# Two attention branches in a hybrid block: row blocks of four first-branch and seven second-branch heads issued side by side

## The chip, the cores and the metric

The kernel runs on one core of a Trainium2 chip. The engines of the core are named as the profile names them: PE (TensorE, matrix products into PSUM), DVE (VectorE), ACT (ScalarE, functions by table and copies), POOL (GpSimd) and SP (SyncE, which here only issues DMAs). Each engine works through its own instructions in a fixed order; waits between engines are semaphores. The metric is the device time in microseconds.

## The reference

One layer on 2048 frames of 1024 channels. After a norm and one wide projection, two attention branches run on the same input: stick-breaking attention (first branch, "sb") and latent attention with softmax (second branch, "mla"), 8 heads each. Sigmoid gates merge them.

```
h = rmsnorm(x, norm_in_g[l]);  proj = h @ w_in[l]     # split into nine parts
# first branch, 8 heads of 64:
z = q_sb k_sb^T * scale
log_beta = log_sigmoid(z);  log_1m = where(strict, log_sigmoid(-z), 0)
later = cumsum(log_1m, reverse=True) - log_1m
o_sb = where(strict, exp(log_beta + later), 0) @ v_sb
# second branch, 8 heads of 96 (64 and 32 rotated), values of 64:
p = softmax(where(allowed, z, -inf));  o_mla = p @ v_mla
y = g_sb * ((o_sb * silu(gate_sb)) @ w_o_sb) + g_mla * ((o_mla * silu(gate_mla)) @ w_o_mla)
out = rmsnorm(x + y @ w_out)
```

## The kernel before

Frames are taken in reverse order, in 16 row blocks of 128, so a row block `i` attends to the 16 - i key blocks from i on (`chunks`: one chunk of up to 1024 keys for i of 8 and more, two chunks before that). Every factor of a matmul is split into a high and a low half of 16 bits, and a product is three matmuls (`gemm`).

The work has four kinds.

- *Norms.* `norm_x` brings x, scales it, splits it and turns it by a DMA transpose into hT, which stays in SBUF as two halves (big0, big1).
- *Dense steps.* `dense_stream` is a generator of 224 steps, each one row block of one 384-column piece of the wide projection (24 matmuls into a PSUM tile mm of a ring of two): four pieces for the first branch's heads (sb), the second branch's queries (mq) and keys (mk) with a second, smaller product each (up-projection), and eight gate pieces (g). The weights of a piece are prepared ahead (`prep_w`, `bound_of`), with a round trip through DRAM for a maximum. When mk is done, its row buffers are closed and their memory becomes the pool `more`.
- *Heads.* `sb_units` computes, for each chunk, scores z (PSUM, two tiles of 1024 columns), two Sigmoids on ACT into U and B, a running product over U on DVE (`stick`, one chunk late), their product into B, then in `weigh` the high and low halves into a tile hl, a DMA transpose of hl into hlT, and values on PE one chunk late (two, once `more` is open: `run_third`). `mla_units` computes scores once for the row maximum, once turned with the maximum taken off, Exp on ACT into U or B, halves into a tile pt, and values. pt shares the rings of hl and hlT.
- *Closing stage.* `gated`, `merge` and `finish`, for 16 row blocks: gates, the two output products, the last product (1536 matmuls of 512 columns in all) and the last norm. Its weights `W["o"]` and `W["w"]` are split by `resident` into the places of the two halves of hT.

The order: 16 dense steps with the norms, then the 16 heads one after another, the first branch's eight first. `PLAN` says how many dense steps a head carries, spread over its row blocks:

```
PLAN = [17] * 8 + [8] * 7 + [4]
```

So the first branch's heads carry 136 steps and the second's 60; 12 are left, and are written behind the heads. This is the order in which the program is written. A scheduler then sets the order in which each engine's instructions stand, within the limits of buffers and dependencies, and can move a step forward. POOL issues the gate stores (`gd<-go`, a ring of two go tiles) and clears the first column of every U.

Where ACT goes from Sigmoid to Exp or back, the built program has an instruction ACT_TABLE_LOAD in between.

Of the kernel before, what the change touches and what calls it, by code (L numbers as in the profile page):

```python
# [9 lines left out]
F32 = mybir.dt.float32  # L10
# [6 lines left out]
P = 128  # L17
S = 2048
# [13 lines left out]
MASK = -3.0e35  # L32
PLAN = [17] * 8 + [8] * 7 + [4]
SCALES = ("g", 4)
# [5 lines left out]
def block_kernel(tc, x, norm_in_g, w_in, w_ck, b_gate, q_norm_g, w_q_up, kv_norm_g, w_kv_up,  # L40
# [11 lines left out]
    with ExitStack() as ctx:  # L52
# [131 lines left out]
        with ExitStack() as tctx:  # L184
# [26 lines left out]
            def u_tile():  # L211
                return un.tile([P, 1028], F32, name="U", tag="U")

            def b_tile():
                return un.tile([P, 1024], F32, name="B", tag="B")

            def hl_tile(n):
                count[0] += 1
                pool, bufs = (more[0], 2) if more and count[0] % 5 % 2 == 0 else (un, 2)
                return pool.tile([P, 2048], F16, name="hl", tag="hl", bufs=bufs)[:, 0:2 * n]  # L220

            def hlT_tile():
                pool, bufs = (more[0], 3) if more and count[0] % 5 % 2 == 0 else (un, 2)
                return pool.tile([P, 16, 128], F16, name="hlT", tag="hlT", bufs=bufs)

            def norm_x(i):
                xt = (b_tile() if i % 2 else u_tile())[:, 0:1024]
                SP.dma_start(out=xt, in_=x[i * P:(i + 1) * P, :])
                hl = (hlT_tile().rearrange("p a c -> p (a c)") if i % 2 else hl_tile(1024))
# [51 lines left out]

            def weigh(unit, vt, blk0, n, first, last, fill, done):


                run_third(2 if more else 1)
                hl = hl_tile(n)
                fill(hl[:, 0:n], hl[:, n:2 * n])
                nb = n // P
                t = hlT_tile()
                SP.dma_start_transpose(out=t[:, 0:2 * nb, :], in_=hl)  # L290
# [18 lines left out]
            def o_group(col):  # L309

                cur = {}

                def put(av, f, i):
                    if i % 4 == 0:
                        cur["t"] = kvp.tile([P, 4, 64], F32, name="ot", tag="ot", bufs=2)
# [6 lines left out]
            def halves(nm, *parts):  # L322

                out = []
                for a in range(2):
                    t = kvp.tile([P, 8, 130 if nm == "vt" else 128], F16, name=nm, tag=nm, bufs=3)
# [30 lines left out]
            def sb_units(h, pre):  # L357
# [4 lines left out]
                for i in range(NB):  # L362
# [5 lines left out]
                    for ci, (c0, n) in enumerate(cks):  # L368
# [8 lines left out]
                        def stick(U=U, B=B, n=n, ci=ci, c0=c0, i=i, unit=unit, last=(ci == len(cks) - 1)):  # L377
                            V.tensor_tensor_scan(out=U[:, 0:n + 1], data0=U[:, 0:n + 1], data1=U[:, 0:n + 1],  # L378
                                                 initial=unit["prev"] if ci else PS, op0=ALU.mult, op1=ALU.bypass)
                            unit["prev"] = U[:, n:n + 1]  # L380
                            V.tensor_tensor(out=B[:, 0:n], in0=B[:, 0:n], in1=U[:, 0:n], op=ALU.mult)  # L381
# [4 lines left out]

                            weigh(unit, vt, i + c0 // P, n, ci == 0, last, fill, lambda av: put(av, of, i))

# [155 lines left out]

            pt_count = [0]

            def pt_tile():

                pt_count[0] += 1
                k = pt_count[0] % (9 if more else 4)  # L550
                if k < 4:
                    pool, tag, bufs = un, "hl" if k % 2 else "hlT", 2
                else:
                    pool, tag, bufs = (more[0], "hl", 2) if k % 5 < 2 else (more[0], "hlT", 3)
                return pool.tile([P, 16, 128], F16, name="pt", tag=tag, bufs=bufs)

            lift, turn, last_av = deque(), deque(), deque()
# [11 lines left out]
            def mla_units(h, pre):  # L569
                mzc = pre[8]  # L570
                kh = halves("kt", (0, 64, mk_d[0:64, :, h, :]), (64, 128, mk_d[0:64, :, 8, :]))
                kl = halves("kl", (0, 64, mk_d[64:128, :, h, :]), (64, 128, mk_d[64:128, :, 8, :]))
                vt = halves("vt", (0, P, mv_d[:, :, h, :]))
                put = o_group(512 + h * 64)
                for i in range(NB):
                    if i % 4 == 0:
                        qt4 = kvp.tile([P, 2, 4, 128], F16, name="qt", tag="qt", bufs=2)
# [16 lines left out]
                    def row_max(mr=mr, qh=qh):  # L594

                        mt = ps_av()
                        with tc.issue_after(last_pe[0].ins):
# [3 lines left out]
                    def weights(i=i, cks=cks, qh=qh, ql=ql):  # L601
                        parts = []
                        for ci, (c0, n) in enumerate(cks):
# [258 lines left out]
            for i in range(NB):  # L862
                advance(1)
                if i + LEAD < NB:
                    norm_x(i + LEAD)
            for h in range(2 * H):
                if h == 2 * H - 1:
                    mla_stages(0, 0)
                    mla_stages(0, 0)
                    mctx.close()  # L870
                    more.clear()
                    tl.append(tctx.enter_context(tc.tile_pool(name="tl0", bufs=1, side="right", reuse_waits="tile")))
                if h == H:
                    run_second(0)
                    run_third(0)
                it = sb_units(h, pre["sb", h // 2]) if h < H else mla_units(h - H, pre["mk", 0])
                tot = sum(S - i * P for i in range(NB))
                cum, done = 0, 0
                for i, _ in enumerate(it):
                    cum += S - i * P  # L880
                    want = PLAN[h] * cum // tot
                    advance(want - done)
                    done = want
                    if h == 2 * H - 1 and i == EARLY:
                        gated(0)

# [73 lines left out]
```

## Time and profile before

| | |
|---|---|
| median of three runs | 2286.37 us (2282.97 to 2297.44) |
| the profiled execution | 2291.27 us |
| its span in the trace | 2289.5 us |
| mean granted clock of PE | 0.956 of full |
| busy: PE, DVE, ACT | 86%, 68%, 55% |

"Busy" is the time in which an instruction of that engine is under way. Matmuls are pipelined, so one that takes 0.33 us from start to end can start 0.16 us after the one before. At 1.00 of the clock PE runs at 2.4 GHz, at half of it at 1.2 GHz.

### The profile page before, as it was taken

To read this page: it belongs to the slowest core of one execution; us is meant where nothing else is said; L and a number is where in the kernel's file an instruction comes from. 1 tells how busy PE (TensorE), PEld (TensorE's weight loads), DVE (VectorE), ACT (ScalarE), POOL (GpSimd) and SP (SyncE) were. 2 spreads that over 40 slices of the span, in tenths; PEclk is the share of its full clock that TensorE was granted. 3 is DMA by queue.
4 is the path that set the end of the run, shared out by engine and by line. 5 is a ranking of instruction groups with operands and counts; after the bars stand their busy time and mean duration, and the time that the engine had idled before them with its cause. 6 is when DMAs were issued, how large, how long until landed. Compare 5 with 4: busy or idle time off the path is not lost.

```text
span 2289.5 us, 46188 instructions
## 1 busy us (share of the span) xinstructions
PE 1967.3 (86%) x18656; PEld 1252.5 (55%) x18656; DVE 1557.9 (68%) x2500; ACT 1265.4 (55%) x2116; POOL 277.8 (12%) x690
## 2 busy tenths in 40 slices
PE   3878888788767887999899999968999787999997
PEld 1545555445435544555557676755767675444443
DVE  3368778668766869887885554765565876766674
ACT  6456566555545657776654643775544777322321
POOL 1211111111111111112110101001010000000000
PEclk9989999999979999999999999998999998999999
DMA  9979888897988979888771522243252323866752
GB/s 249 225 132 156 157 153 160 160 153 159 185 167 157 207 169 169 172 158 168 130 173 48 149 63 72 61 125 87 63 149 67 110 71 80 256 194 185 200 157 74
DMA packets 666150, 330.21 MB, mean 144 GB/s; under 512 B 605776, under 2 KB 626000, under 8 KB 663888
## 3 DMA queue, kind: packets, MB, share of 16 engines
q1 hardware_dynamic: 645392, 272.19, 56.1%
q0 software_dynamic: 18432, 54.55, 8.5%
q8 instruction: 146, 2.39, 0.5%
q10 hardware_dynamic: 2112, 0.52, 0.1%
q14 instruction: 68, 0.56, 0.1%
HBM read 132.06 MB, written 71.90 MB: 89 GB/s over the span
## 4 chain that ended last, share of the span: by engine, by line
PE 47%; DMA 23%; DVE 13%; ACT 8%; issue 6%; SPq 1%; POOL 1%; ACTq 0%; DVEq 0%; POOLq 0%
DMA hlT<-hl 7%; PE mm L178 7%; PE mm L180 6%; PE mm L179 6%; PE z L344 4%; DVE U L378 4%; DMA rt<-r 3%; PE yo L178 2%; PE z L609 2%; PE yo L180 2%; PE yo L179 2%; PE z L613 2%; PE z L612 2%; DMA utb<-hlb 2%; PE y L178 2%
## 5 line engine op out<-in xcount | busy, mean ns | idle before, releaser
L178 PE MATMUL mm<-w,hT 128*128 128x384 f16 (+1 forms) x1792 | 590.2, 330 | 79.5 <-ACT w L166 37.0
L179 PE MATMUL mm<-w,hT 128*128 128x384 f16 (+1 forms) x1792 | 589.4, 329 | 0.8 <-DVE w L167 0.8
L180 PE MATMUL mm<-w,hT 128*128 128x384 f16 (+1 forms) x1792 | 589.0, 329 | 0.0
L378 DVE TENSOR_TENSOR_SCAN U<-U 128x1025 f32<-128x1025 f32 (+3 forms) x192 | 323.7, 1687 | 51.0 <-ACT U L374 49.5
L344 PE MATMUL z<-kt,qt 128*128 128x512 f16 x960 | 257.6, 362 | 58.4 <-DVE rt L432 13.2
L384 ACT CAST hl<-B 128x1024 f16<-128x1024 f32 (+3 forms) x192 | 152.4, 798 | 234.0 <-DVE B L381 131.2
L178 PEld LDWEIGHTS <-hT 128*128 128x128 f16 x1792 | 178.5, 100 | 155.7 <-DMA hT<-hl 25.3
L179 PEld LDWEIGHTS <-hT 128*128 128x128 f16 x1792 | 178.3, 99 | 148.4 <-issue 48.6
L180 PEld LDWEIGHTS <-hT 128*128 128x128 f16 x1792 | 178.3, 99 | 113.0 <-issue 9.2
L385 DVE TENSOR_TENSOR hl<-B,hl 128x1024 f16<-128x1024 f32 (+3 forms) x192 | 173.5, 909 | 87.9 <-ACT hl L384 87.4
L609 PE MATMUL z<-qt,kt 128*128 128x128 f16 x1088 | 205.0, 224 | 19.6 <-DVE mx L587 14.8
L587 DVE TENSOR_REDUCE mx<-z 128x1 f32<-128x1024 f32 (+3 forms) x192 | 173.6, 909 | 70.4 <-PE z L348 49.8
L613 PE MATMUL z<-qt,kl 128*128 128x128 f16 x1088 | 202.0, 224 | 0.0
L612 PE MATMUL z<-qt,kt 128*128 128x128 f16 x1088 | 202.0, 224 | 0.0
L299 PE MATMUL av<-vt,hlT 128*128 128x64 f16 x1088 | 124.4, 198 | 89.5 <-DMA hlT<-hl 87.3
L374 ACT ACTIVATE U<-z,nzc 128x1024 f32<-128x1024 f32 (+3 forms) x192 | 166.4, 867 | 39.4 <-PE z L344 38.7
L381 DVE TENSOR_TENSOR B<-B,U 128x1024 f32<-128x1024 f32 (+3 forms) x192 | 174.7, 912 | 15.6 <-ACT B L375 1.2
L375 ACT ACTIVATE B<-z,zc 128x1024 f32<-128x1024 f32 (+3 forms) x192 | 166.1, 867 | 3.1 <-DVE hl L385 3.0
L299 PEld LDWEIGHTS <-hlT 128*128 128x128 f16 x1088 | 103.8, 100 | 116.7 <-DMA hlT<-hl 106.8
L619 DVE SCALAR_TENSOR_TENSOR pt<-U,pt 128x1024 f16<-128x1024 f32 (+7 forms) x128 | 96.5, 755 | 90.4 <-ACT pt L618 89.8
L344 PEld LDWEIGHTS <-qt 128*128 128x128 f16 x960 | 87.3, 101 | 102.4 <-issue 45.1
L628 PE MATMUL av<-vt,pt 128*128 128x65 f16 x1088 | 127.0, 194 | 10.2 <-ACT qt L599 4.2
(258 smaller groups left out, 4367.2 us busy)
## 6 DMA issues: line engine op xcount, KB each, us to landing
gd<-go POOLq DMA_DIRECT2D x128, 192.0 KB, 3.3
wf<-in_w_in_dram SPq DMA_DIRECT2D x26, 768.0 KB, 5.6
gt<-gd SPq DMA_DIRECT2D x10, 1024.0 KB, 6.0
qkd<-rt POOLq DMA_DIRECT2D x32, 256.0 KB, 4.5
mqd<-rt SPq DMA_DIRECT2D x32, 256.0 KB, 2.7
qt<-mqd POOLq DMA_DIRECT2D x32, 256.0 KB, 3.5
wf<-in_w_out_dram SPq DMA_DIRECT2D x16, 512.0 KB, 4.2
xt<-in_x_dram SPq DMA_DIRECT2D x16, 512.0 KB, 3.6
```

Of the source, the lines that this page charges most:

```text
L178: T.matmul(out=ps, lhsT=xh(k), rhs=wh(k), start=(k == 0), stop=False)
L179: T.matmul(out=ps, lhsT=xh(k), rhs=wl(k), start=False, stop=False)
L180: last_pe[0] = T.matmul(out=ps, lhsT=xl(k), rhs=wh(k), start=False, stop=(k == kk - 1))
L299: T.matmul(out=av[:, 0:64], lhsT=t[:, j, :], rhs=v[:, 0:64], start=(first and j == 0), stop=False)
L344: last_pe[0] = T.matmul(out=z[:, s:s + c], lhsT=st, rhs=half[:, o + s // P:o + (s + c) // P, :].rearrange("p a b -> p (a b)"), start=(a == ...
L378: V.tensor_tensor_scan(out=U[:, 0:n + 1], data0=U[:, 0:n + 1], data1=U[:, 0:n + 1], initial=unit["prev"] if ci else PS, op0=ALU.mult, op1= ...
L381: V.tensor_tensor(out=B[:, 0:n], in0=B[:, 0:n], in1=U[:, 0:n], op=ALU.mult)
L385: V.tensor_tensor(out=lo, in0=B[:, 0:n], in1=hi, op=ALU.subtract)
L587: V.tensor_reduce(out=mx[:, ci:ci + 1], in_=z[:, 0:n], axis=AX.X, op=ALU.max)
L609: T.matmul(out=zj, lhsT=kh[b // 8][:, b % 8, :], rhs=qh, start=True, stop=False)
L612: T.matmul(out=zj, lhsT=kh[b // 8][:, b % 8, :], rhs=ql, start=False, stop=False)
L613: T.matmul(out=zj, lhsT=kl[b // 8][:, b % 8, :], rhs=qh, start=False, stop=True)
```

## The change

The heads are written in three stages in place of one list. Four first-branch heads run alone with 80 dense steps. After them the dense stream is advanced until `more` is open. Then the row blocks of the other four first-branch heads and of seven second-branch heads alternate, with 108 dense steps: `spread` takes the next row block from the stream that has done the smaller share of its work. The last second-branch head follows alone with four dense steps. 15 steps are written behind it.

To make room, the halves of the first branch's weights no longer have a tile hl: they lie over U, which is spent by then (1028 floats hold 2 x 1024 halves), so U stays in use until its transpose has landed. U has four buffers instead of three. Since U is overwritten, the last element of the running product is copied to a small tile pv for the next chunk. Turned tiles have two tags, hlT and pt, of two buffers each: alternating when one branch runs alone, one for each branch side by side. Values are two chunks late in the stage alone and one chunk late side by side (the reverse of before). The second branch's keys, values and queries come from `more` while both run, and the last head's low key halves lie over a U tile. `row_max` takes its PSUM tile from the dense steps' ring mm.

```diff
-PLAN = [17] * 8 + [8] * 7 + [4]
+ALONE, ALONE_STEPS = 4, 80
+BOTH_STEPS = 108
+LAST_STEPS = 4
...
-                return un.tile([P, 1028], F32, name="U", tag="U")
+                return un.tile([P, 1028], F32, name="U", tag="U", bufs=4)
...
+            def turned_tile(sb):
+
+                count[0] += 1
+                tag = ("hlT" if sb else "pt") if stage[0] == "both" else ("hlT", "pt")[count[0] % 2]
+                return un.tile([P, 16, 128], F16, name=tag, tag=tag, bufs=2)
...
-            def weigh(unit, vt, blk0, n, first, last, fill, done):
-
-
-                run_third(2 if more else 1)
-                hl = hl_tile(n)
+            def weigh(unit, hl, vt, blk0, n, first, last, fill, done):
+
+
+                run_third(1 if stage[0] == "both" else 2)
                 fill(hl[:, 0:n], hl[:, n:2 * n])
                 nb = n // P
-                t = hlT_tile()
+                t = turned_tile(True)
...
-                            unit["prev"] = U[:, n:n + 1]
+                            if not last:
+                                unit["prev"] = sm.tile([P, 1], F32, name="pv", tag="pv", bufs=3)
+                                V.tensor_copy(out=unit["prev"], in_=U[:, n:n + 1])
...
-                            weigh(unit, vt, i + c0 // P, n, ci == 0, last, fill, lambda av: put(av, of, i))
+                            weigh(unit, U.bitcast(F16)[:, 0:2 * n], vt, i + c0 // P, n, ci == 0, last, fill,
+                                  lambda av: put(av, of, i))
...
-                        mt = ps_av()
+                        mt = ps_mm()
...
-                            pt = pt_tile()
+                            pt = turned_tile(False)
...
-            for h in range(2 * H):
...
+            def heads(units, hs, key):
+                for h in hs:
+                    for i, _ in enumerate(units(h, pre[key(h)])):
+                        yield work(i)
+
+            def spread(streams, steps):
+
+
+                done, total, gone = [0] * len(streams), sum(t for _, t in streams), 0
+                while True:
+                    left = [k for k, (_, t) in enumerate(streams) if done[k] < t]
+                    if not left:
+                        break
+                    k = min(left, key=lambda k: done[k] / streams[k][1])
+                    done[k] += next(streams[k][0])
+                    want = steps * sum(done) // total
+                    advance(want - gone)
+                    gone = want
+                    yield
+                for it, _ in streams:
+                    next(it, None)
+
+            sb_key, mla_key = (lambda h: ("sb", h // 2)), (lambda h: ("mk", 0))
+            for _ in spread([(heads(sb_units, range(ALONE), sb_key), ALONE * whole)], ALONE_STEPS):
+                pass
+            while not more:
+                advance(1)
+            stage[0] = "both"
+            for _ in spread([(heads(sb_units, range(ALONE, H), sb_key), (H - ALONE) * whole),
+                             (heads(mla_units, range(H - 1), mla_key), (H - 1) * whole)], BOTH_STEPS):
+                pass
...
+            for i, _ in enumerate(spread([(heads(mla_units, [H - 1], mla_key), whole)], LAST_STEPS)):
+                if i == EARLY:
+                    gated(0)
```

What the scheduler makes of it is shown at three places. The first is SP, in the middle of the first-branch heads that run beside the projections (hl or U holds the halves, hlT and pt are turned tiles, rt belongs to the projections). Before:

```order
L290 DMA_TRANSPOSE hlT<-hl 128x14x128
L290 DMA_TRANSPOSE hlT<-hl 128x16x128
L445 DMA wf<-in_w_q_up_dram 128x3x384 x2
L290 DMA_TRANSPOSE hlT<-hl 128x12x128
L263 DMA_TRANSPOSE rt<-r 128x8x128
```

After:

```order
L290 DMA_TRANSPOSE pt<-U 128x16x128
L332 DMA vt<-vd_77 128x8x128
L290 DMA_TRANSPOSE hlT<-U 128x14x128
L264 DMA_TRANSPOSE rt<-r 128x8x128
L135 DMA wjunk<-bd_cq 128x128
L290 DMA_TRANSPOSE pt<-U 128x12x128
```

Four turned tiles take turns instead of two, and the source is U itself. The second place is ACT in the gate steps. Before, in a first-branch head, it has Sigmoids (U and B from z), the cast of the high half, the copy of an output (ot) and gate work (go, wjunk):

```order
L374 ACTIVATE U<-z,nzc_1387 128x1024
L375 ACTIVATE B<-z,zc_1386 128x1024
L384 CAST hl<-B 128x1024
L374 ACTIVATE U<-z,nzc_1387 128x768
L156 ACTIVATE wjunk,am<-wf 128x768
L384 CAST hl<-B 128x896
L317 ACTIVATE ot<-av,of_1388 128x64
L661 ACTIVATE go<-mm,gt_7989 128x384
```

After, side by side (the scale mzc marks the second branch's Exp, nzc and zc the Sigmoids):

```order
L378 ACT_TABLE_LOAD
L378 ACTIVATE U<-z,nzc_1287 128x896
L379 ACTIVATE B<-z,zc_1286 128x896
L662 ACTIVATE go<-mm,gt_9002 128x384
L600 CAST qt<-mm 32x128
L158 ACTIVATE wjunk,am<-wf 128x768 x2
L616 ACT_TABLE_LOAD
L616 ACTIVATE U<-z,mzc 128x768
L390 CAST U<-B 128x896
```

Sigmoid and Exp now alternate, each with its table load; the whole program has 112 of them, and had 8. The third place is ACT at the end of the heads, where the last weights (WHL from in_w_out, scale r_wout) are split. Before, they stand among the second branch's Exps:

```order
L172 ACTIVATE WHL_26363<-wf,r_wout 128x1024 x2
L615 ACTIVATE U<-z,mzc 128x1024
L599 CAST qt<-av 32x128
L317 ACTIVATE ot<-av,fo 128x64
L618 ACTIVATE pt<-U 128x1024
L615 ACTIVATE U<-z,mzc 128x896
L172 ACTIVATE WHL_26363<-wf,r_wout 128x1024
```

After:

```order
L806 ACT_TABLE_LOAD
L806 ACTIVATE gt<-gt 128x1024
L810 ACTIVATE gt<-gt 128x2048
L174 ACTIVATE WHL_26298<-wf,r_wout 128x1024 x2
L806 ACTIVATE w<-w 128x3072
L174 ACTIVATE WHL_26298<-wf,r_wout 128x1024 x4
L174 ACTIVATE w<-w,ra 128x1024
```

They moved behind the last Exp, between the gates of the closing stage's first blocks (gt and w). On PE the last 309 matmuls before the closing stage are dense steps in one row; before, the last dense step stood ahead of more than 1,900 matmuls of the heads.

## Rows read from the trace of the kernel before

**Rows 1.** The page's first part: busy us, share of the span, instructions.
```profile
PE 1967.3 (86%) x18656; PEld 1252.5 (55%) x18656; DVE 1557.9 (68%) x2500; ACT 1265.4 (55%) x2116; POOL 277.8 (12%) x690
```

**Rows 2.** Timeline of PE, two fed stretches: start us, duration us, instruction.
```profile
1612.18 0.33 PE L180 MATMUL mm<-w,hT 128*128 128x384 f16 x1
1612.35 0.33 PE L178 MATMUL mm<-w,hT 128*128 128x384 f16 x1
1612.51 0.19 PE L630 MATMUL av<-vt,pt 128*128 128x65 f16 x1
1612.54 0.19 PE L628 MATMUL av<-vt,pt 128*128 128x65 f16 x1
1612.57 0.19 PE L629 MATMUL av<-vt,pt 128*128 128x64 f16 x1
...
2040.22 0.38 PE L180 MATMUL yo<-WHL,utb 128*128 128x512 f16 x1
2040.44 0.38 PE L178 MATMUL yo<-WHL,utb 128*128 128x512 f16 x1
```

**Rows 3.** Stretches: us, busy PE, PEld, DVE, ACT, POOL, clock, DMA share, GB/s.
```profile
100.00:820.00 720.00, 584.85 (x4843) 356.80 (x4842) 521.25 (x856) 407.74 (x760) 123.33 (x331) 0.93 0.85 162
820.00:1190.00 370.00, 323.82 (x3029) 202.75 (x3029) 309.81 (x344) 255.16 (x426) 64.00 (x187) 0.95 0.87 166
1190.00:1450.00 260.00, 256.94 (x2994) 185.03 (x2992) 140.76 (x255) 121.59 (x203) 26.68 (x49) 1.00 0.30 82
1450.00:1600.00 150.00, 116.00 (x1784) 94.52 (x1782) 95.50 (x201) 108.26 (x193) 10.40 (x16) 0.93 0.37 95
1600.00:1760.00 160.00, 159.15 (x1912) 116.11 (x1911) 95.73 (x166) 79.76 (x124) 17.29 (x30) 1.00 0.32 98
1760.00:1950.00 190.00, 154.68 (x2352) 124.47 (x2350) 139.76 (x258) 142.55 (x225) 6.57 (x12) 0.93 0.33 89
1950.00:2290.00 340.00, 318.61 (x1464) 142.64 (x1462) 214.96 (x338) 91.51 (x89) 8.81 (x16) 0.98 0.62 175
```

**Rows 4.** Stretches of tile mm (dense), then of tile hlT (first-branch values): PE first.
```profile
100.00:820.00 720.00, 362.82 (x2108) 51.78 (x133) 63.19 (x151) 0.93 0.85 162
820.00:1190.00 370.00, 221.55 (x1269) 10.29 (x24) 25.30 (x46) 0.95 0.87 166
...
100.00:820.00 720.00, 76.42 (x1842) 70.05 (x1842) 0.00 (x0) 0.00 (x0) 0.93 0.85 162
820.00:1190.00 370.00, 59.06 (x1404) 54.52 (x1404) 0.00 (x0) 0.00 (x0) 0.95 0.87 166
```

**Rows 5.** Waits from 100 to 600 us, then 820 to 1190: total us, times, longest.
```profile
ACT hl L384 <- DMA hlT<-hl: 90.2, 32, 7.7
...
PE av L299 <- DMA hlT<-hl: 53.9, 31, 5.8
...
PE av L299 <- DMA hlT<-hl: 33.4, 17, 5.1
...
ACT hl L384 <- DMA hlT<-hl: 5.1, 2, 4.2
```

**Rows 6.** Two short stretches, columns as in rows 3.
```profile
600.00:680.00 80.00, 49.16 (x362) 29.01 (x358) 53.24 (x133) 40.14 (x87) 8.65 (x31) 0.81 0.81 168
920.00:1000.00 80.00, 73.16 (x722) 46.73 (x720) 73.47 (x78) 63.15 (x106) 13.48 (x42) 0.98 0.82 165
```

**Rows 7.** The page's DMA issues: count, median us to landing.
```profile
hlT<-hl SPq DMA_TRANSPOSE x192, 4.8
```

**Rows 8.** Groups on DVE by form: count, busy us, mean ns, idle before.
```profile
L589 DVE TENSOR_TENSOR mx<-mx 128x1 f32<-128x1 f32 x64 | 9.8, 153 | 0.5
```

**Rows 9.** Timeline of ACT around one table load: start us, duration us.
```profile
1902.98 1.06 ACT L618 ACTIVATE pt<-B 128x1024 f16<-128x1024 f32 x1
1904.06 1.28 ACT L615 ACT_TABLE_LOAD   x1
1905.35 0.37 ACT L615 ACTIVATE U<-z,mzc 128x128 f32<-128x128 f32 x1
```

**Rows 10.** Tile WHL: duration ns min/median/max, first and last start us.
```profile
L172 ACT ACTIVATE WHL<-wf,r_wout x8: 1134/1148/1152, 1776.6 to 1799.7; 128x1024 f16<-128x1024 f32 x8
```

More of the change, by code (lines that the diff above doesn't have):

```diff
@@ L211, in u_tile @@
             def u_tile():
-                return un.tile([P, 1028], F32, name="U", tag="U")
+                return un.tile([P, 1028], F32, name="U", tag="U", bufs=4)
             def b_tile():
                 return un.tile([P, 1024], F32, name="B", tag="B")
-            def hl_tile(n):
+            stage = ["alone"]
+            def turned_tile(sb):
                 count[0] += 1
[L219 to L224, printed above, removed]
+                tag = ("hlT" if sb else "pt") if stage[0] == "both" else ("hlT", "pt")[count[0] % 2]
+                return un.tile([P, 16, 128], F16, name=tag, tag=tag, bufs=2)
             def norm_x(i):
@@ L228, in norm_x @@
                 SP.dma_start(out=xt, in_=x[i * P:(i + 1) * P, :])
-                hl = (hlT_tile().rearrange("p a c -> p (a c)") if i % 2 else hl_tile(1024))
+                hl = turned_tile(True).rearrange("p a c -> p (a c)")
                 ssq = sm.tile([P, 1], F32, name="ssq", tag="ssq")
@@ L314, in put @@
                     if i % 4 == 0:
-                        cur["t"] = kvp.tile([P, 4, 64], F32, name="ot", tag="ot", bufs=2)
+                        tag = "ot" if col < 512 else "om"
+                        cur["t"] = kvp.tile([P, 4, 64], F32, name=tag, tag=tag, bufs=2)
                     o = cur["t"][:, i % 4, :]
@@ L320, in o_group, with halves @@
                 return put
-            def halves(nm, *parts):
+            def halves(nm, *parts, pool=None, places=None):
                 out = []
                 for a in range(2):
-                    t = kvp.tile([P, 8, 130 if nm == "vt" else 128], F16, name=nm, tag=nm, bufs=3)
+                    if places:
+                        t = places[a]
+                    else:
+                        t = (pool or kvp).tile([P, 8, 130 if nm[0] == "v" else 128], F16, name=nm, tag=nm, bufs=3)
                     for p0, p1, src in parts:
@@ L543, in mk_project @@
                     yield
[L545 to L555, printed above, removed]
             lift, turn, last_av = deque(), deque(), deque()
@@ L570, in mla_units @@
                 mzc = pre[8]
-                kh = halves("kt", (0, 64, mk_d[0:64, :, h, :]), (64, 128, mk_d[0:64, :, 8, :]))
-                kl = halves("kl", (0, 64, mk_d[64:128, :, h, :]), (64, 128, mk_d[64:128, :, 8, :]))
-                vt = halves("vt", (0, P, mv_d[:, :, h, :]))
+                alone = h == H - 1
+                pool = kvp if alone else more[0]
+                places = None
+                if alone:
+                    two = u_tile().bitcast(F16)[:, 0:2048].rearrange("p (a k c) -> p a k c", a=2, k=8)
+                    places = [two[:, 0], two[:, 1]]
+                kh = halves("kt" if alone else "kh", (0, 64, mk_d[0:64, :, h, :]), (64, 128, mk_d[0:64, :, 8, :]), pool=pool)
+                kl = halves("kl", (0, 64, mk_d[64:128, :, h, :]), (64, 128, mk_d[64:128, :, 8, :]), pool=pool, places=places)
+                vt = halves("vt" if alone else "vm", (0, P, mv_d[:, :, h, :]), pool=pool)
                 put = o_group(512 + h * 64)
@@ L576, in mla_units @@
                     if i % 4 == 0:
-                        qt4 = kvp.tile([P, 2, 4, 128], F16, name="qt", tag="qt", bufs=2)
+                        qt4 = pool.tile([P, 2, 4, 128], F16, name="qt", tag="qt" if alone else "qm", bufs=2)
                         qm = qt4.rearrange("p a i c -> p (a i c)").rearrange("p (i a c) -> p i a c", i=4, a=2)
@@ L865, in block_kernel, with work @@
                     norm_x(i + LEAD)
-            for h in range(2 * H):
[L867 to L885, printed above, removed]
+            def work(i):
+                return S - i * P
@@ new lines, in block_kernel @@
+            whole = sum(work(i) for i in range(NB))
+            def heads(units, hs, key):
[16 more added lines that the diff above has]
+                    next(it, None)
@@ L887, in block_kernel @@
+            run_second(0)
+            run_third(0)
+            mla_stages(0, 0)
+            mla_stages(0, 0)
+            mctx.close()
+            stage[0] = "last"
+            tl.append(tctx.enter_context(tc.tile_pool(name="tl0", bufs=1, side="right", reuse_waits="tile")))
+            for i, _ in enumerate(spread([(heads(mla_units, [H - 1], mla_key), whole)], LAST_STEPS)):
+                if i == EARLY:
+                    gated(0)
             mla_stages(0, 0)
```

## The prediction

> **What bounds the kernel now.** I read the page's first lines, then the busy time of each engine by stretch, then the spacing of TensorE's matmuls inside a stretch that never waits. PE is busy 86% of the span [rows 1], but that word hides its pace, so I price PE by spacing. At full clock a 384-column matmul starts 0.16 us after the one before, a 512-column one 0.215 us, a 128-column one, in proportion, 0.055 us, and a value matmul of 64 or 65 columns 0.03 us [rows 2]. From the code's counts (136 key blocks a head, three value matmuls each) this gives the work of each piece, with decimals kept:
> - a dense step, 24 matmuls of 384 columns: 3.9 us; one of the 288-column block, in proportion, 2.9 us; the two up-projections together 88 us
> - a first-branch head: scores over 2 x 17,408 columns 14.7 us, masks 0.9, values 408 x 0.030 = 12.2, so 27.8 us
> - a second-branch head: scores for the maximum 7.3, turned scores 408 x 0.055 = 22.6, small ones 2.0, values 12.2, so 44.1 us
> - the closing stage, 1536 matmuls of 512 columns: 332 us.
>
> 224 dense steps (208 x 3.9 + 16 x 2.9 = 858), 88, 8 x 27.8, 8 x 44.1 and 332 make some 1855 us. The span is 2289.5 us, so about 435 us pass without PE at its full pace.
>
> By stretch [rows 3]: from 1190 to 1450 us and from 1600 to 1760 us second-branch heads run with dense steps, PE is busy 99% at clock 1.00, and DVE and ACT are about half idle. From 1760 to 1950 us such heads run without dense steps: PE is busy 155 of 190 us at clock 0.93. From 100 to 820 us four and a half first-branch heads (1842 value matmuls / 408) run beside the first projections: 2108 dense matmuls x 0.1625 less 16 for the narrow ones, 83 us of up-projection and 4.51 x 27.8 make 536 us of work in 720 us, a PE share of 0.745. From 820 to 1190 us 1269 such matmuls (a few too narrow or wide) and 3.44 heads make 307 us in 370 us, a share of 0.83, with DVE at 0.84 and DMA at 0.87 [rows 3, 4]. There PE and ACT wait for the turned weights: before 600 us PE waits 53.9 us for hlT and ACT 90.2 us for a place of hl; after 820 us, with the second pair of buffers and values two chunks late, it is 33.4 and 5.1 us [rows 5].
>
> **The change part by part.** PE's work is the same, matmul for matmul; what moves is which waits stand beside it. I add up the new stages.
>
> *Before 100 us*: first norms and dense steps, as before: 100 us.
>
> *Four first-branch heads alone*, with 80 dense steps and one more: 48 x 3.9 + 16 x 3.9 + 16 x 2.9 + 88 + 4 x 27.8, and 18 for what of the first block is left at 100 us, make 515 us. The high half now lies in U, so hl's ring of two is gone; values come two chunks late and turned tiles alternate between two tags, as the order on SP shows. That is what the kernel before did only after 820 us. Bounds are therefore the shares 0.745 (nothing gained) and 0.83: 691 and 620 us. I take 0.79, midway, 652 us: the projections with chains of their own, and the weight preparation that sank PE to 49 of 80 us after 600 us [rows 6], stay. U now lives until its transpose has landed (4.8 us median [rows 7]); the ring of four replaces three. If that cover fails, the memset of U's first column waits on POOL, and queued behind it are the gate stores (later on), whose ring of two go tiles holds back the next dense step. The memset waits for the transpose of four tiles earlier; in the order about 10 us of ACT's own work stand between a cast and that reuse, against 0.9 + 4.8 us needed, so I cost it at nothing.
>
> *Four first-branch and seven second-branch heads side by side*, with 108 gate steps: 4 x 27.8 + 7 x 44.1 + 108 x 3.9 = 841 us of PE. ACT: 255 us for 3.44 heads and the steps beside them gives 297 for four; the four stretches from 1190 to 1950 us hold 452 us for eight second-branch heads, so 396 for seven; less about 10 for steps counted twice, 683 us. DVE likewise 360 + 413 - 10 = 763 us, and some 5 us for 32 copies of the running product (the nearest row is an operation on one column, 0.15 us [rows 8]). New on ACT: Sigmoid and Exp alternate, and the built program holds 112 loads of ACT's function table where there were 8. One load takes 1.28 us; the instruction ahead ends 0.02 us before it, and the next begins 0.01 us behind it [rows 9]. So 104 x 1.28 = 133 us, all but a few here, and ACT reaches 816 us. The Trainium skill ("ScalarE: Activation LUTs", What ACT_TABLE_LOAD costs) says that a switch costs 2.66 us, since a drain of 1.38 us goes with the load, and its section on table sets tells one to do all calls of a set before switching, which speaks against this change. By that price the sum on ACT would be 683 + 104 x 2.66 = 960 us, and the stage at the share taken below 1129 us. The rows here show no drain beside the load.
>
> PE 841, ACT 816, DVE 768: no engine leads, each waits for the others, and z has two buffers for three kinds of chunk. The share PE reaches in such a mix I take from stretches: 0.83 from 820 to 1190 us with DVE 0.84, ACT 0.69; 0.99 (busy) from 1190 to 1450 us where the others are half idle; lower from 1760 to 1950 us, where ACT and DVE are at 0.75 and no dense step fills in. The best 80 us (920 to 1000 us) reach DVE 0.92, ACT 0.79 and PE busy 0.91 [rows 3, 6]. The bounds are 0.78 and 0.92, 1078 and 914 us. I take 0.85, 989 us, nearest to 820 to 1190 us: DMA, at 0.87 there, now carries half as many transposes per microsecond, and every unit has a dense step to fill it, but ACT has 133 us more. Row_max takes the dense steps' PSUM ring: 128 short uses, hidden unless ACT is late with the copy.
>
> *The last second-branch head* keeps four dense steps: 44 + 16 = 60 us at about 0.75 (the busy share of 1760 to 1950 us times its clock, 0.81 x 0.93), 80 us. The other 15 dense steps now stand behind it, 58 us at full pace. *Handover*: the last weights are split into the place of the second half of hT, free only after the last dense step. Before, those eight pieces took 24 us on ACT, from 1776.6 us on, under the heads [rows 10]; in the new order they stand behind every Exp, and the second block's own split is queued behind six of them: 18 us to its turn, some 12 to the landing of its transpose, against 10.4 us of the first merge (48 x 0.216): 20 us exposed. Together 158 us.
>
> *Closing stage*: 332 us, and the 24 us that it loses now between 1950 us and the end (1464 x 0.216 = 316 of 340): 356 us.
>
> Sum: 100 + 652 + 989 + 158 + 356 = 2255 us of span, 2257 us with the 1.8 us around it, against 2291.3 us of the profiled execution. That execution lies 4.9 us above the median of the three runs, so the forecast is **2252 us**, 1.5% below 2286.4.
>
> **The rivals.**
> - *Slower: ACT's queue takes over.* The loads stand in front of the Exp or Sigmoid that frees z, on the in-order queue of an engine at 97% of PE's work; PE's order is fixed, so a late z holds the dense steps behind it too. For it: without dense steps, ACT and DVE at 0.75 already drag PE. Against it: mm has its own ring. At a share of 0.78 the stage takes 1078 us and the kernel 2341 us; below 0.80 it is over 1% slower.
> - *A switch costs its drain as well.* If each load, among queued work, makes ACT wait as long again, ACT holds 683 + 2 x 133 = 949 us, leads, and at 0.85 the stage takes 1116 us: 2379 us. The load row speaks against it [rows 9]; the other seven loads before are alike. The Trainium skill ("ScalarE: Activation LUTs", What ACT_TABLE_LOAD costs) states such a drain.
> - *The first stage gains nothing* (0.745): DMA at 0.85 and the preparation chains bind, not the buffers: 39 us more, 2291 us, no change. That the streams don't interleave is excluded by the order.
> - *Faster: two branches cover each other fully.* 0.92 side by side and 0.83 alone: 75 + 32 us less, 2145 us. For it: 920 to 1000 us. Against it: such stretches are short.
>
> **How the numbers follow.** Chances: forecast 0.43 (some 2210 to 2290 us), ACT's queue 0.24, the drain 0.04, no gain in the first stage 0.12, faster 0.17. The range leaves out the drain and the outer ends of ACT's queue and of the fast case: 2155 to 2345 us. About 1% is what a measurement of this kernel can tell from no change. Of the forecast 0.31 lies beyond it; with the fast case 0.48 faster; 0.22 same, from the rest of the forecast and most of the third case; 0.30 slower.
>
> **What would show it.** In the new profile: ACT loses about 133 us to 112 table loads of 1.28 us; waits of ACT for hlT nearly vanish before the first Exp, which comes near 750 us instead of 1206; the side-by-side stage lasts about 990 us with DMA near half; a dense-only stretch of 50 us at clock 1.00 stands before the closing stage, and a gap of about 20 us after it. I am wrong if the side-by-side stage runs below 0.80 or above 0.90 of PE's pace, or if the first Exp comes after 800 us.

## The result and the profile after

The changed kernel takes **2367.43 us** (median of four runs, 2357.92 to 2369.64) against 2289.55 us (four runs, 2282.97 to 2297.44) for the kernel before on the same chip: a ratio of 1.0331, 95% interval 1.0285 to 1.0377. It is 3.3% slower; the forecast was 2252 us, 1.5% faster. The profiled execution has a span of 2363.8 us.

The first part of its page, as in [rows 1]:

```profile
PE 1981.7 (84%) x18656; PEld 1263.8 (53%) x18656; DVE 1554.1 (66%) x2564; ACT 1397.6 (59%) x2220; POOL 276.0 (12%) x690
```

PE does the same matmuls, DVE has 64 short instructions more in the same busy time, and ACT has 132 us and 104 instructions more. The groups of ACT from 830 to 1850 us (busy us, mean ns, idle before) show what they are:

```profile
L616 ACT ACTIVATE U<-z,mzc 128x768 f32<-128x768 f32 (+3 forms) x107 | 79.3, 741 | 39.9 <-PE z L614 38.7
...
L616 ACT ACT_TABLE_LOAD x53 | 68.0, 1283 | 1.0
L378 ACT ACT_TABLE_LOAD x52 | 66.7, 1283 | 0.9
```

The loads are as long as in [rows 9]. ACT sat idle for only 1.9 us ahead of all 105: a load does not wait for the scores, it starts as soon as its turn comes. The Exp or Sigmoid behind it does wait for them.

Stretches of the new kernel, columns as in [rows 3]: the heads alone, side by side, the dense-only steps, the closing stage.

```profile
100.00:808.00 708.00, 586.83 (x4768) 358.43 (x4767) 511.34 (x896) 399.29 (x757) 127.15 (x330) 0.93 0.93 170
808.00:1905.00 1097.00, 929.38 (x11378) 674.92 (x11377) 729.27 (x1153) 804.97 (x1219) 111.12 (x278) 0.95 0.43 100
...
1940.00:2003.00 63.00, 62.46 (x374) 36.20 (x372) 18.04 (x27) 11.39 (x9) 7.55 (x14) 1.00 0.48 167
2060.00:2364.00 304.00, 286.00 (x1313) 128.15 (x1311) 186.31 (x292) 78.14 (x77) 8.21 (x15) 0.98 0.60 164
```

A stretch's share is PE's work in it, priced by the prediction's spacing, over its length. The 4768 matmuls of the first row are 545 us of work, a share of 0.77, and the 11378 of the second 858 us, a share of **0.782**. The dense-only row loses nothing. The first Exp comes behind a load at 808.1 us, the first start in this row of line 616 (ns each, first and last start us):

```profile
L616 ACT ACT_TABLE_LOAD  x55: 1283/1283/1283, 808.1 to 1902.6; - x55
```

PE's waits from 830 to 1850 us (total us, times, longest):

```profile
PE z L348 <- ACT B L379: 32.2, 26, 4.0
PE z L348 <- DVE mx L588: 26.1, 18, 3.6
PE z L348 <- ACT U L616: 16.8, 13, 3.2
PE z L610 <- ACT U L616: 16.0, 10, 3.8
PE av L299 <- DMA hlT<-U: 10.6, 3, 7.0
PE z L610 <- DVE mx L588: 10.5, 10, 3.4
PE z L348 <- ACT B L616: 8.5, 5, 3.1
PE z L610 <- ACT B L379: 7.5, 6, 2.1
```

The waits for turned weights of [rows 5] have shrunk; PE now waits for a score tile z that ACT has not read yet (the five lines with ACT: 81.0 us). A stretch of ACT's timeline (start us, duration us) shows why:

```profile
1210.28 0.47 ACT L662 ACTIVATE go<-mm,gt 128x256 f32<-128x256 f32 x1
1210.76 1.28 ACT L378 ACT_TABLE_LOAD   x1
1212.05 0.37 ACT L378 ACTIVATE U<-z,nzc 128x128 f32<-128x128 f32 x1
1212.32 0.36 ACT L379 ACTIVATE B<-z,zc 128x128 f32<-128x128 f32 x1
```

The load comes directly ahead of the two reads that give z back, and holds it 1.28 us longer. Of the 109 loads from 808 us on, 108 have a read of z right behind them, and 95 of these reads begin within 0.05 us of the load's end: their scores were there already.

### The profile page after: what moved, and what is told of

Same layout as the page of the kernel before. It is cut to its first block, busy times and chain, and to the rows that moved or that the text cites. A ratio compares the mean times of both kernels' runs of the same rounds, so it can differ in the third digit from the quotient of the medians.

```text
span 2363.8 us, 46263 instructions
## 1 busy us (share of the span) xinstructions
PE 1981.7 (84%) x18656; PEld 1263.8 (53%) x18656; DVE 1554.1 (66%) x2564; ACT 1397.6 (59%) x2220; POOL 276.0 (12%) x690
## 4 chain that ended last, share of the span: by engine, by line
PE 30%; ACT 15%; DVE 10%; DMA 6%; issue 5%; SPq 0%; another core or an unknown queue 0%; POOL 0%; DVEq 0%; ACTq 0%; POOLq 0%
DVE U L382 4%; PE mm L180 4%; PE mm L181 4%; PE mm L182 4%; ACT U L378 2%; ACT L378 2%; PE yo L180 2%; PE yo L182 2%; PE yo L181 2%; PE y L180 2%; ACT pt L619 2%; PE y L181 2%; ACT U L616 2%; PE y L182 2%; PE z L610 2%
## 5 line engine op out<-in xcount | busy, mean ns | idle before, releaser
L390 ACT CAST U<-B 128x1024 f16<-128x1024 f32 (+3 forms) x192 | 153.0, 798 | 184.0 <-DVE B L387 145.1
L382 DVE TENSOR_TENSOR_SCAN U<-U 128x1025 f32<-128x1025 f32 (+7 forms) x128 | 173.7, 1357 | 84.0 <-ACT U L378 74.0
L610 PE MATMUL z<-qt,kh 128*128 128x128 f16 x952 | 181.6, 226 | 39.6 <-ACT U L616 16.0
L348 PE MATMUL z<-kt,qt 128*128 128x512 f16 (+3 forms) x680 | 170.8, 353 | 49.9 <-ACT B L379 29.4
L391 DVE TENSOR_TENSOR U<-B,U 128x1024 f16<-128x1024 f32 (+3 forms) x192 | 174.0, 907 | 52.2 <-ACT U L390 51.0
L614 PE MATMUL z<-qt,kl 128*128 128x128 f16 x952 | 179.4, 227 | 0.0
L613 PE MATMUL z<-qt,kh 128*128 128x128 f16 x952 | 179.3, 227 | 0.0
L666 POOL DMA_DIRECT2D gd<-go x128 | 70.0, 547 | 812.2 <-DVE go L664 368.0
L382 DVE TENSOR_TENSOR_SCAN U<-U,pv 128x1025 f32<-128x1025 f32 x64 | 150.3, 2349 | 16.7 <-ACT U L378 15.7
L620 DVE SCALAR_TENSOR_TENSOR pt<-U,pt 128x1024 f16<-128x1024 f32 (+3 forms) x124 | 93.8, 756 | 95.3 <-ACT pt L619 94.9
L348 PE MATMUL z<-kh,qt 128*128 128x512 f16 (+2 forms) x280 | 82.1, 367 | 88.3 <-ACT B L379 30.0
```

The lines of the kernel that those rows point to most:

```text
L348: last_pe[0] = T.matmul(out=z[:, s:s + c], lhsT=st, rhs=half[:, o + s // P:o + (s + c) // P, :].rearrange("p a b -> p (a b)"), start=(a == ...
L391: V.tensor_tensor(out=lo, in0=B[:, 0:n], in1=hi, op=ALU.subtract)
L610: T.matmul(out=zj, lhsT=kh[b // 8][:, b % 8, :], rhs=qh, start=True, stop=False)
L613: T.matmul(out=zj, lhsT=kh[b // 8][:, b % 8, :], rhs=ql, start=False, stop=False)
L614: T.matmul(out=zj, lhsT=kl[b // 8][:, b % 8, :], rhs=qh, start=False, stop=True)
```

## The experiments

Theory T1: the loads cost the side-by-side stage its share, because they stand ahead of the reads of z. Rival T2: three nearly equally loaded engines, tied together by two score tiles, reach no more than 0.78 anyway, and the loads are incidental. For the first stage: S1, the transposing DMA is its bound (busy 0.93); S2, the chains of projections and preparation are. Between calls the median of the kernel before moved from 2285.7 to 2289.6 us, so differences between kernels of different calls are good to some 4 us.

**No loads side by side** (e1_one_table).

```
-  A.activation(out=E[:, 0:n], in_=z[:, 0:n], func=AF.Exp, scale=mzc)
+  A.activation(out=E[:, 0:n], in_=z[:, 0:n], func=AF.Sigmoid, scale=mzc)
```

> The second branch's weights are computed with a sigmoid in place of the exponential (so its output is another one); ScalarE then reads one function table in the side-by-side stage, and the 109 table loads of 1283 ns in it are gone (140 us of ScalarE's queue). All else is the changed kernel's. Theory T1 (the loads stand in ScalarE's in-order queue ahead of the reads that free the score tiles z, and cost the stage its share): the stage's share of TensorE work goes from 0.78 to 0.85 to 0.88, 1092 us become 970 to 1005, total 2260 to 2290. Theory T2 (three nearly equally loaded engines are tied together by two score tiles; the loads are incidental): the stage keeps 0.77 to 0.80, total 2340 to 2370.

2264.37 us (2263.14 to 2268.62), ratio to before 0.99 (0.9882 to 0.9917). The reads take as long as with Exp (739 against 741 ns). The stage, and PE's waits from 830 to 1750 us:

```profile
808.00:1800.00 992.00, 890.27 (x11310) 651.10 (x11310) 719.33 (x1142) 655.23 (x1101) 111.17 (x277) 0.98 0.49 108
```
```profile
PE z L348 <- DVE mx L588: 20.8, 19, 2.4
...
PE z L348 <- ACT B L379: 10.5, 11, 2.2
...
PE z L610 <- ACT U L616: 7.6, 8, 1.9
PE z L348 <- ACT B L616: 6.3, 6, 2.7
...
PE z L610 <- ACT B L616: 2.9, 5, 0.8
```

The stage reaches 851 us of work in 992, a share of 0.858; the waits for ACT in the lines shown fall from 81.0 to 27.3 us. Over the two whole stages (1097 and 992 us) PE's waits for z on ACT are 86 and 32 us, those on DVE 40 and 32. T2 is out: without the loads, the mix of engines gives the share that was forecast.

**The new buffers, heads in turn** (e2_in_turn).

```
-  ... spread([(heads(sb_units, range(ALONE), sb_key), ALONE * whole)], ALONE_STEPS)
-  ... spread([(heads(sb_units, range(ALONE, H), ...)), (heads(mla_units, range(H - 1), ...))], BOTH_STEPS)
-  while not more: advance(1)
-  stage[0] = "both"
+  ... spread([(heads(sb_units, range(H), sb_key), H * whole)], 136)
   run_second(0); run_third(0)
+  ... spread([(heads(mla_units, range(H - 1), mla_key), (H - 1) * whole)], 56)
```

> The changed kernel's buffers (the first branch's split lies over its U tile, four U tiles, the turned tiles under two names) with the heads in turn again: eight first-branch heads with 136 dense steps behind them, then seven second-branch heads with 56, the last with 4. Theory T1 and T2 alike (the side-by-side order costs the time, the buffers do not): 2260 to 2300, one table load at the change of branch. Rival (the split over its own U tile holds the tile until the transposing DMA has read it, and so slows every first-branch head): the first branch's stretch stays as long per head as in the changed kernel's alone stage or longer, total 2330 or more.

2287.98 us (10 runs, 2283.08 to 2296.44), ratio 0.9998 (0.9982 to 1.0014). The split over U, the four U tiles and the new tags are neutral over the whole kernel; the rival of the ring of U tiles is out. They are not neutral within it: by the spacing PE has 604 us of work behind it at 820 us where the kernel before had 584, 899 against 891 at 1190 us and 1538 against 1536 at 1950 us. What gives the early gain back was not tested. With e1 this splits the result: buffers 0, side-by-side order without loads about -24 us, loads about +103 us.

**Bursts of eight row blocks** (e3_bursts).

```
-  k = min(left, key=lambda k: done[k] / streams[k][1])
+  if turns % BURST == 0 or k not in left:
+      k = min(left, key=lambda k: done[k] / streams[k][1])
+  turns += 1
```

> The side-by-side stage takes eight row blocks of one branch and then eight of the other, in place of changing at almost every row block; the same work, some 14 table loads in the stage in place of 109. T1 (the loads cost the stage its share): 60 to 100 us less, 2265 to 2305. T2 or a cost of bursts (a burst of the first branch is limited by its transposing DMA and a burst of the second by TensorE, so that nothing hides the one behind the other): 2340 to 2400.

2345.94 us (2342.88 to 2353.53), ratio 1.0258 (1.0234 to 1.0282): only 21 us less, though 15 loads are left in place of 109. That is outside T1's range, and inside the one for a cost of bursts. Its largest waits of PE from 830 to 1850 us:

```profile
PE av L300 <- DMA hlT<-U: 65.7, 33, 10.7
PE z L349 <- ACT B L380: 19.4, 19, 3.2
```

The wait for z has shrunk as T1 says, but the wait for turned weights has grown from 10.6 to 65.7 us: eight first-branch row blocks in a row have nothing between a transpose and its use. Here the fine interleaving hides the transposes, and the loads are its price.

**Half of the transposes' bytes** (e4_half_turned).

```
-  SP.dma_start_transpose(out=t[:, 0:2 * nb, :], in_=hl)
+  SP.dma_start_transpose(out=t[:, 0:nb, :], in_=hl[:, 0:n])
-  T.matmul(out=av[:, 0:64], lhsT=t[:, nb + j, :], ...)
+  T.matmul(out=av[:, 0:64], lhsT=t[:, j, :], ...)
```

> The first branch's weights are turned for the high half alone (half the bytes of each transposing DMA); the low matmuls read the high half's turned tile, so the output lacks the low half. Theory S1 (in the alone stage, 100 to 808 us, the transposing DMA is the bound: DMA share 0.93): the first table load for the exponential comes at 730 to 760 us in place of 808, total 2300 to 2320. S2 (the dense projections' and preparation's chains bound that stage): it stays at 795 to 810, total 2355 to 2370.

2352.14 us (2341.9 to 2357.54): 15 us less, and the first Exp at 793 us, between the two theories' ranges. The stage alone:

```profile
100.00:808.00 708.00, 603.06 (x4935) 369.51 (x4934) 518.40 (x912) 413.07 (x780) 126.04 (x335) 0.93 0.74 147
```

DMA falls from 0.93 to 0.74 and PE starts 167 matmuls more in the same 708 us, a share of 0.79 in place of 0.77. The DMA is a part of what holds that stage, not its bound. S1 falls for the most part; that S2 is right was not shown by itself.

**Copies in place of loads** (e5_copies_for_loads), on top of e1:

```
+  def stand_in(kind):
+      if drawn[0] != kind:
+          for _ in range(2):
+              pin(A.activation(out=wjunk[:, 256:896], in_=wjunk[:, 256:896], func=AF.Copy, scale=1.0))
+          drawn[0] = kind
```

It is called ahead of both branches' reads of z; clearing wjunk at the start is left out here.

> The kernel with the sigmoid in the second branch (no table loads side by side), with two dummy copies of 640 columns on ScalarE ahead of the scores' reads wherever the stream changes: 107 pairs, some 1.3 us each by the rows of the 1024-column Square (1056 ns), so about the ScalarE time of the 109 loads. T1 in the form that a load costs the time it takes in the queue and no more: 2340 to 2375, as the changed kernel. T1 in the form that a load costs more than its own 1283 ns (what was running before it has to end first): 2290 to 2325.

2314.57 us (2311.67 to 2323.02): 50 us over e1, half of what the loads cost, though ACT's busy time grew by 128 us (1253.7 to 1381.5). By the expectation that would make a load more costly than an instruction of its length. ACT's timeline shows another reason:

```profile
1220.26 0.31 ACT L328 ACTIVATE om<-av,fo 128x64 f32<-128x64 f32 x1
1220.45 0.74 ACT L227 ACTIVATE wjunk<-wjunk 128x640 bf16<-128x640 bf16 x1
1221.08 0.32 ACT L631 ACTIVATE pt<-U 128x128 f16<-128x128 f32 x1
1221.28 0.74 ACT L227 ACTIVATE wjunk<-wjunk 128x640 bf16<-128x640 bf16 x1
1221.90 1.01 ACT L389 ACTIVATE U<-z,nzc 128x896 f32<-128x896 f32 x1
...
1223.68 0.76 ACT L227 ACTIVATE wjunk<-wjunk 128x640 bf16<-128x640 bf16 x1
1224.46 0.26 ACT L611 CAST qt<-mm 32x128 f16<-32x128 f32 x1
```

The scheduler split pairs: of the 214 copies, 94 have a read of z right behind them (or behind the next copy), and 120 have other work. So the run measured the same time partly at other places, and did not settle the price; e10 below does.

**Reads twice** (e10_reads_twice), on top of e1:

```
+  for _ in range(times("mla", ci)):      # 2 where the stream changes, on the first chunk
       A.activation(out=E[:, 0:n], in_=z[:, 0:n], func=AF.Sigmoid, scale=mzc)
```

and the same for the two reads of the first branch.

> The kernel with the sigmoid in the second branch (no loads side by side), in which ScalarE repeats the score reads of a row block's first chunk wherever the stream changes: the same instruction twice in a row, some 54 + 108 reads of 0.74 and 0.85 us, about 130 us of ScalarE, and all of it stands where a load stood, before the score tile is given back. If what counts is that the time lies on the way to the release of z: 2345 to 2375, as the changed kernel. If a table load costs by itself more than an instruction of its length: 2300 to 2330, as the copies.

2354.5 us (2353.13 to 2355.77): 90 us over e1 for 103 us of ACT's busy time, in the range of T1: what counts is the time on the way to the release of z, and a load does not cost more than reads of its length. The two are not quite alike, since a load can start before the scores are there and a repeated read cannot. The largest wait of PE from 830 to 1780 us is the one for z again:

```profile
PE z L355 <- ACT B L389: 51.3, 27, 5.2
```

The same stretch in the changed kernel, with the copies (e5) and with the reads twice:

```profile
808.00:1845.00 1037.00, 876.37 (x10628) 633.50 (x10627) 689.99 (x1081) 763.38 (x1154) 108.96 (x274) 0.95 0.44 101
808.00:1845.00 1037.00, 904.87 (x11294) 657.04 (x11293) 723.39 (x1143) 782.80 (x1316) 111.94 (x277) 0.97 0.48 104
808.00:1845.00 1037.00, 883.45 (x10722) 639.45 (x10721) 697.86 (x1094) 731.25 (x1225) 111.89 (x274) 0.95 0.46 101
```

ACT is busiest with the copies (783 us against 763 and 731), yet PE starts the most matmuls there (11294 against 10628 and 10722). How full ACT is does not decide; what stands behind the added time does.

**The same loads in the kernel before** (e7_loads_in_turn).

```
+  if ci == 0 and i % 2 == 0 and h < H - 1:
+      pin(A.activation(out=tiny, in_=eye[:, 0:1], func=AF.Sigmoid))
   A.activation(out=E[:, 0:n], in_=z[:, 0:n], func=AF.Exp, scale=mzc)
```

> The kernel before, with a one-column sigmoid on ScalarE ahead of the exponential in every other row block of the second branch's first seven heads (its result is read by nothing): 110 more table loads, 141 us more on ScalarE, in a stretch of 760 us in which ScalarE is busy 0.59 of the time and TensorE 0.90. If a load costs because it stands ahead of a score's read in the queue, wherever ScalarE's share stands: +80 to +110, 2370 to 2400. If it costs only where ScalarE, VectorE and TensorE are all near their limits, as side by side: +0 to +35, 2290 to 2325.

2374.42 us (2371.65 to 2381.26), ratio 1.0398 (1.0364 to 1.0433): 89 us for 110 loads, in second-branch heads with no first-branch head beside them, where ACT was busy 0.59 of the time before. With the loads it is busy 0.71 of it (607 of 850 us), as in the changed kernel's stage (0.73), so this run shows that the cost does not need the two branches side by side; that place and not fullness decides rests on e5 and e10. PE's first wait from 1190 to 2040 us:

```profile
PE z L345 <- ACT U L618: 24.6, 21, 4.0
```

In all, PE's waits for z on ACT grew from 12 to 55 us, and its waits for the tiles pt and qt from ACT, which free no z, from 9 to 32 us: a load also delays other work behind it in the queue.

**Half of the loads** (e8_half_loads).

```
-  func=AF.Exp
+  func=AF.Exp if h % 2 else AF.Sigmoid
```

> The changed kernel with the exponential in the second branch's heads 1, 3 and 5 and a sigmoid in heads 0, 2, 4 and 6 (so these heads' output is another one): 50 table loads in the program in place of 112. T1 with the cost in proportion to the loads (103 us for 109): 2305 to 2325, with the lost time of TensorE alternating by head. If the cost sets in only from a certain share of ScalarE on: 2265 to 2290.

2304.46 us (2295.14 to 2310.03): 40 us over e1 for 48 loads more in the program (50 against 2), 0.84 us each; the 110 of the changed kernel cost 0.94 each. About in proportion, at the lower end of what was expected; no threshold shows between none, half and all of the loads. By the spacing the share alternates with the heads, as expected: 0.79, 0.77 and 0.75 in the three stretches with loads (935 to 1072, 1225 to 1383 and 1524 to 1675 us), 0.84 to 0.91 before, between and behind them.

**Tanh in both stages** (e6_tanh).

```
-  A.activation(out=U[:, 1:n + 1], in_=z[:, 0:n], func=AF.Sigmoid, scale=nzc)
-  A.activation(out=B[:, 0:n], in_=z[:, 0:n], func=AF.Sigmoid, scale=zc)
+  A.activation(out=B[:, 0:n], in_=z[:, 0:n], func=AF.Tanh, scale=zc)      # zc is half of what it was
+  A.activation(out=U[:, 1:n + 1], in_=B[:, 0:n], func=AF.Copy, scale=-0.5, bias=0.5)
-  V.tensor_tensor(out=B[:, 0:n], in0=B[:, 0:n], in1=U[:, 0:n], op=ALU.mult)
+  V.scalar_tensor_tensor(out=B[:, 0:n], in0=B[:, 0:n], scalar=1.0, in1=U[:, 0:n], op0=ALU.add, op1=ALU.mult)
```

The scan starts at PS / 2.

> The first branch takes its two sigmoids from one tanh: B = tanh(z/2) read from the score tile, U = 0.5 - 0.5 B read from B, and VectorE's product becomes (B + 1) U with the scan started at half its value. ScalarE still has two instructions to a chunk, and the program holds 4 table loads in place of 112, since tanh and exp come in one table (the Trainium skill, ScalarE: Activation LUTs, Table sets, lists tanh in the set of exp too). T1: as the sigmoid kernel, 2250 to 2280, which is faster than the kernel before. A rival: B waits for nothing new but U now comes after B, and the longer chain to the scan takes 10 to 30 us back: 2280 to 2300.

2288.31 us (10 runs, 2279.28 to 2293.97), ratio 1.0006 (0.9985 to 1.0027): the loads are gone (4 left), yet it is 24 us slower than e1. By the spacing, side by side has a share of 0.86, as in e1, but from 100 to 808 us 534 us of work are done where e1 did 548. The rival is right, and at one place only, the first stage. That the cause there is the chain to the scan, longer by one step on ACT, was the expectation; it was not tested apart from the tanh itself.

**Tanh only side by side** (e9_tanh_side_by_side): heads 0 to 3 keep their Sigmoids.

```
+  both = h >= ALONE        # tanh, copy and (B + 1) U as above; else the two sigmoids
```

> The first branch's heads 0 to 3 keep their two sigmoids (no exponential runs beside them); heads 4 to 7 take theirs from the tanh, so that side by side only tanh, exp and copies run; 6 table loads in the program. If the 24 us between the tanh kernel (2288) and the sigmoid kernel (2264) are the longer chain in the alone stage (at 800 us the tanh kernel had 14 us less TensorE work behind it, and side by side both had a share of 0.86): 2260 to 2272, about 1% under the kernel before. If the tanh costs side by side too: 2280 to 2292.

**2264.93 us** (6 runs, 2255.89 to 2267.8), ratio to before 0.9893 (0.9859 to 0.9927): 1.1% faster than the kernel before and 4.3% faster than the changed one, with the reference's result computed in full. Its page and its side-by-side stage:

```profile
PE 1958.8 (86%) x18656; PEld 1249.3 (55%) x18656; DVE 1546.6 (68%) x2564; ACT 1258.4 (56%) x2114; POOL 278.0 (12%) x690
```
```profile
808.00:1808.00 1000.00, 906.13 (x11433) 660.26 (x11432) 725.92 (x1158) 667.59 (x1119) 116.32 (x279) 0.98 0.51 109
```

It starts 11433 matmuls in 1000 us; the changed kernel needed 1097 us for 11378. With the Sigmoids back in heads 0 to 3 the 24 us of e6 are gone, so they lay in these heads.

## Why the prediction was wrong

**The step that failed** is the share of the side-by-side stage: 0.85 was taken, 0.782 came, the lower bound and the first rival's value. Both signs of being wrong that the prediction named came: a share below 0.80, and a first Exp after 800 us. By equal work: at 1905 us PE has 1446 us of work behind it (43 before 100 us, 545, 858). The prediction's stages hold 48 (as the kernel before at 100 us) + 515 + 841, and 42 of the last head's 60, at 100 + 652 + 989 + 56 = 1797 us. Of these 108 us late, 27 were there at 808 us (588 us of work, forecast for 752 + 25/0.85 = 781), and 81 arose side by side.

The sum on ACT in that step was right: 816 us forecast, 805 us busy in the 1097 us of the stage, the loads 140 of them. What failed is the argument from the sum. It set 816 against 841 us of PE, found that no engine leads, and so priced the loads at nothing but a somewhat smaller margin. ACT never became the bound (0.73 busy). The loads cost because of where they stand: behind the score matmuls and ahead of the read that gives one of two z tiles back. The first rival named that place, and said 2341 us; its other premise, a queue nearly as full as PE's work, is not what decides: with the copies ACT was busy for longer than in the changed kernel, at half the cost. The runs give the price by place, as time added per microsecond of ACT's added busy time (against e1, the last against the kernel before):

| added on ACT | busy us | time us | per us |
|---|---|---|---|
| loads of the changed kernel | 143.9 | 103.1 | 0.72 |
| half of them | 61.5 | 40.1 | 0.65 |
| reads twice, ahead of z's release | 102.8 | 90.1 | 0.88 |
| copies, 120 of 214 elsewhere | 127.8 | 50.2 | 0.39 |
| loads in the kernel before | 151.1 | 88.7 | 0.59 |

**What was right.** Without loads the stage runs at 0.858 (e1) and 0.860 (e9), so 0.85, taken from the stretch of 820 to 1190 us, fits these engines without the loads; the prediction had meant it with them. The drain rival is out: 109 of the changed kernel's 112 loads begin within 0.03 us of the end of the instruction ahead, 95 of the 108 reads follow a load at once, and a repeated read at the same place costs more per microsecond than a load, so nothing beyond the load's 1283 ns has to be assumed. The Trainium skill ("ScalarE: Activation LUTs", What ACT_TABLE_LOAD costs) gives 2.66 us for a switch, a drain included; no run here shows the drain, and the loads cost 0.81 to 0.94 us each. The rule of the Trainium skill ("ScalarE: Activation LUTs", Table sets) to do all calls of one set before switching holds here for whole branches: the same buffers with the heads in turn take 2288 us where the alternation takes 2367 (e2). For bursts of eight row blocks it gave back 21 us (e3).

**The first stage**: a share of 0.77 where 0.79 was taken (708 us for its 545 us of work; at 0.79, 690), 18 of the 27 us that were missing at 808 us. The first Exp came 58 us later than forecast mainly because 30 us more of PE's work lay ahead of it than the step counted, work that was then missing behind it. The waits did go from where they were: ACT's 90.2 us for hl [rows 5] have no successor of that size, and PE waits 13.9 us for hlT before 600 us in place of 53.9. The ring of U tiles, which the prediction had costed at nothing, does make POOL wait for the transposes before the memset of U (100 to 808 us):

```profile
POOL U L377 <- DMA hlT<-U: 120.3, 35, 12.4
POOL U L377 <- DMA pt<-U: 105.4, 36, 10.7
```

But POOL had waited at that memset before, for DVE (75.0 and 71.5 us from 100 to 820 us), and little of the new wait reaches ACT's write to U in the same stretch:

```profile
ACT U L378 <- DMA hlT<-U: 5.3, 4, 3.2
...
ACT U L378 <- DMA pt<-U: 2.1, 1, 2.1
```

What POOL's wait costs PE was not shown. The share rose from 0.745 to 0.77, less than a third of the way to 0.83, and over a whole kernel the same buffers gave nothing that can be measured (e2). What holds this stage at 0.77 was not settled: half the transposes' bytes gave 0.79, and the rest stays open.

**The end**: from 1905 us on, 459 us against 458 by the prediction's terms. The dense steps lost nothing in the 63 us of the row above. The handover lay where it was said and was nearly as large, 15.7 us where 20 was forecast: PE's one wait from 2000 to 2025 us.

```profile
PE y L180 <- DMA w<-w: 15.7, 1, 15.7
```

## What to carry to other kernels

An engine's sum tells whether it can be the bound, not what an instruction on it costs: look at what stands right behind the new instruction in its queue, and who waits for that. On the way from PE through ACT's read back to one of two score tiles, time was paid at 0.65 to 0.9 of itself, with ACT idle for a quarter of the stage. Where two streams with different function tables are to be interleaved, first look for functions that share a table (here tanh for sigmoid beside exp); and interleave finely, since coarse bursts uncovered the transposes that the fine order had hidden.

## What the runs showed of the hardware that was not expected

- Tanh, exp and copies run without a load between them: the tanh kernel has 4 loads in all where the sigmoid beside the exponential needed 112. The Trainium skill ("ScalarE: Activation LUTs", Table sets) lists tanh in the set of exp; the trace agrees.
- The waits came with a lower granted clock. Side by side, the changed kernel's 11378 matmuls kept PE busy for 929 us at a granted clock of 0.95, e1's 11310 for 890 us at 0.98 (means over the stage of a clock that is at 2.4 or 1.2 GHz). So of the 105 us between the two stages (1097 and 992 us) some 66 are idle time and 39 busy time. Of the 39, by the spacing 7 are more matmuls, and by an estimate 28 are the clock: 890 us at 0.98 would be 918 us at 0.95.
